# Upward MLP: 112 DMA issues move from SyncE's queue to ScalarE's

## The chip, the core and the metric

One Trainium2 chip, one of its cores. The metric is the device time of one launch in microseconds (us). Every execution is timed; one more is recorded by the hardware profiler, and its trace is what is read here. Engines: PE (TensorE), ACT (ScalarE), DVE (VectorE), POOL (GpSimd) and SP (SyncE, which here only issues DMAs).

## What is computed

A block of two layers on 1024 tokens of width 1024, in float32. Each layer has a mixer (layer 0: gated delta rule beside an RWKV-7 recurrence; layer 1: retention) and an MLP. The change is in the MLP:

```python
D_MODEL, SEQ, DEPTH = 1024, 1024, 2
D_FF = 4 * D_MODEL
...
for layer in range(DEPTH):
    u = rmsnorm(h, norm_mix_pre[layer])
    ...
    h = h + rmsnorm(mix, norm_mix_post[layer])
    u = rmsnorm(h, norm_mlp_pre[layer])
    f = jnp.square(jax.nn.relu(u @ mlp_w_up[layer])) @ mlp_w_down[layer]
    h = h + rmsnorm(f, norm_mlp_post[layer])
```

## The kernel before

Each matrix product of the MLP is made from seven products of half-size blocks instead of eight (a Strassen-Winograd scheme), and each fp32 operand is split in two parts for PE: the high one by a cast on ACT (L1183), the low one by a subtraction on DVE (L1184); three matmuls (L1315 to L1317, or L1467 to L1469) then make one product.

**Up part.** The 4096 columns of the hidden layer are worked in 16 steps p. For the first eight, `begin(p)` runs early, while the mixer before is still ending (this is called the front below): two products on PE, a copy of the first on ACT (L1335, tile x1, stored to `xds[p]`), and Relu and Square of the second on ACT (L1322, L1323), stored by `store(1, p, r)`. Then a loop runs over p in the order 0, 8, 1, 9, ... 7, 15. Each pass loads 1 MB of weights (L1307), makes sums on POOL, five or seven products on PE and sums on DVE (L1382, L1386, L1390, L1397, L1402), and again Relu and Square on ACT. Its results are the left operands of the down part's seven products: number 1, 2 and 4 come straight from ACT's Square; 3, 5, 6 and 7 are sums that POOL makes of them (L1405 to L1411). `store(n, p, r)` writes each to DRAM, 128 x 512 fp32, 256 KB: to `hds[n][p // 2]`, or, for n = 4 in layer 1, to `hq`.

**Down part.** For each product number and h from 0 to 7 it loads a pair of those results (`hds[n][h]`, L1535) and a block of `mlp_w_down` (L1437), splits both, and multiplies on PE. The sum on POOL in `right` (L1431) and the copies and sums in `flush` finish the scheme. The place where the last p of the up part and the first h of the down part overlap is called the seam below. There are two, one per layer: at about 1440 and 2930 us.

**What sets the order.** A scheduler orders the instructions of each engine beforehand; on the chip every engine runs its own stream in order. A DMA is an instruction in the stream of the engine that issues it. It signals one of eight completion semaphores, DMAHW0 to DMAHW7, given out in rotation over all DMAs of the program; a DMA whose semaphore is still in use by the one eight places before waits, on the engine that issues it, until that one has landed. In the kernel before, all stores and loads of the MLP stand in SP's stream.

Of the kernel before, what the change touches and what calls it, by code (L numbers as in the profile page):

```python
# [20 lines left out]
P = 128  # L21
# [88 lines left out]
def hybrid_block_kernel(  # L110
# [20 lines left out]
    PE, ACT, DVE, POOL, SP = nc.tensor, nc.scalar, nc.vector, nc.gpsimd, nc.sync  # L131
# [3 lines left out]
    def mk(pool, shape, tag, dt=F32, **kw):  # L135
        if isinstance(pool, Area):
            return pool.take(shape, tag, dt, **kw)
        uid[0] += 1
        return pool.tile(shape, dt, tag=tag, name=f"{tag}_{uid[0]}", **kw)
# [24 lines left out]
    hds = {n: [mk(dram, [P, 2, HT], f"hd{n}{i}") for i in range(8)] for n in range(1, 8)}  # L164
    hq = mk(dram, [P, 4, 16, P], "hq")
    xds = [mk(dram, [P, HT], f"xd{p}") for p in range(NB)]
# [1030 lines left out]
    def mlp(layer, res, mid, dst, late=()):  # L1197
# [7 lines left out]
        if True:  # L1205
# [92 lines left out]
            def tile_of(p, area):  # L1298

                raw = mk(area, [P, KT, P], "w0")  # L1300
                SP.dma_start(raw, mlp_w_up[layer][:, 2 * P * p : 2 * P * p + P].rearrange("(k p) c -> p k c", p=P))
                return raw[:, 0:4], raw[:, 4:8]

            def quads(p):

                raw = mk(raws, [P, KT, 2 * P], "raw")
                SP.dma_start(raw, mlp_w_up[layer][:, 2 * P * p : 2 * P * (p + 1)].rearrange("(k p) c -> p k c", p=P))  # L1307
                return {f"a{f + 1}{k + 1}": raw[:, 4 * k : 4 * k + 4, P * f : P * f + P] for f in range(2) for k in range(2)}
# [15 lines left out]

            def store(n, p, r):

                if n == 4 and layer:
                    SP.dma_start(hq[:, :, p, :], r.rearrange("p (t c) -> p t c", c=P))
                else:
                    SP.dma_start(hds[n][p // 2][:, p % 2, :], r)  # L1330

            def first_product(w, x, area=None):
                ps = mk(psu, [P, HT], "pu")
                product(ps, operand(w, area), b11, True, False)
                ACT.copy(x, ps)  # L1335
                return ps

            def first_output(p, ps, w, r, area=None):
                product(ps, operand(w, area), b21, False, True)
                squared(r, ps)  # L1340
                store(1, p, r)

            def begin(p, area, ops_area=None):

                wa, wb = tile_of(p, area)
                x = mk(keep, [P, HT], "x1")
                ps = first_product(wa, x, ops_area)
                SP.dma_start(xds[p], x)
                first_output(p, ps, wb, mk(keep, [P, HT], "r"), ops_area)

            firsts = region((88, 104)).area(4)
            for p in range(NB // 2):
                begin(p, firsts, early_ops)
            firsts = region((0, 16)).area(4)
            later = iter(range(NB // 2, NB))
            for t, n in ((4, 2), (5, 1), (6, 1), (7, 0)):
                next(run[t], None)
                for p in range(n):
                    begin(next(later), firsts)
# [5 lines left out]
            for p in ORDER:  # L1365
                q = quads(p)
# [23 lines left out]
                DVE.tensor_tensor(out=r22, in0=u3, in1=b5, op=ALU.add)  # L1390
                squared(r22, r22)
                store(4, p, r22)
                if p >= NB:
                    first_output(p, b1, q["a12"], r11)
                product(b7, operand(q["a22"]), ops["t4"], False, True)
                r12 = mk(res_, [P, HT], "r")
                DVE.tensor_tensor(out=r12, in0=u2, in1=b7, op=ALU.add)  # L1397
                squared(r12, r12)
                store(2, p, r12)
                product(b5, operand(S[:, 3]), ops["b22"], False, True)  # L1400
                r21 = mk(res_, [P, HT], "r")
# [486 lines left out]
```

## Time and profile before

| what | us |
|---|---|
| median of 3 runs | 3277.05 |
| their range | 3265.05 to 3279.01 |
| the profiled execution | 3272.72 |
| its span on the core | 3271.0 |
| PE busy | 3100.0 (95%) |
| DVE busy | 1996.6 (61%) |
| ACT busy | 1307.8 (40%) |
| POOL busy | 1243.3 (38%) |

DMA-issuing instructions are not counted as busy time. A busy PE is one with a matmul in flight; the granted clock says at what speed. An idle time of an engine costs nothing as long as another engine sets the pace, so the stretches are read one by one. The mean rate of all DMA over the span is 126 GB/s; the 40 us rows show how unevenly that is spread.

### The profile page before, as it was taken

How to read it: one execution, taken by the hardware profiler on the slowest of the kernel's cores; microseconds unless marked ns; L12 is line 12 of the kernel's file. 1: busy time of each engine (PE TensorE's matmuls, PEld its weight loads, DVE VectorE, ACT ScalarE, POOL GpSimd, SP SyncE). 2: the span in 40 equal slices, each digit the busy share in tenths (PEclk: the TensorE clock that was granted, in tenths of full speed). 3: DMA queues.
4: the chain of work that ended last, by engine and by line, in shares of the span. 5: the costliest groups of instructions: out<-in, count | busy, mean ns of one | idle time of the engine just before them, and what ended most of it. 6: DMA issues, size and time to landing. Idle time of an engine off the chain costs nothing. (4 is left out here: it accounts for less than half of the span.)

```text
span 3271.0 us, 44331 instructions
## 1 busy us (share of the span) xinstructions
PE 3100.0 (95%) x16424; PEld 2648.7 (81%) x16424; DVE 1996.6 (61%) x3427; ACT 1307.8 (40%) x2336; POOL 1243.3 (38%) x1549
## 2 busy tenths in 40 slices
PE   8889899899999889999999999999999989999998
PEld 6678787788788668878888899998999878877886
DVE  6445446555534865557578665667655675558585
ACT  5332333332323655544345333234432355553343
POOL 1664354454350067756150111112011057657060
PEclk9898879998979889999999999999999999999999
DMA  5221222221323545585354322344222456566354
GB/s 171 68 58 47 56 72 60 61 63 41 78 77 121 193 138 184 188 293 189 111 173 162 103 78 84 91 136 135 78 84 84 125 172 208 178 244 219 99 165 142
DMA packets 395609, 411.13 MB, mean 126 GB/s; under 512 B 69120, under 2 KB 303488, under 8 KB 394880
## 3 DMA queue, kind: packets, MB, share of 16 engines
q1 hardware_dynamic: 395392, 408.29, 39.7%
q8 instruction: 129, 2.11, 0.3%
q14 instruction: 88, 0.72, 0.1%
HBM read 312.28 MB, written 95.94 MB: 125 GB/s over the span
## 5 line engine op out<-in xcount | busy, mean ns | idle before, releaser
L185 PE MATMUL bank<-piece,piece 128*128 128x512 f32 (+7 forms) x10032 | 1740.7, 335 | 66.1 <-ACT piece L312 14.1
L185 PEld LDWEIGHTS bank<-piece,piece 128*128 128x128 f32 (+1 forms) x10032 | 1501.9, 199 | 273.2 <-issue 34.6
L1184 DVE TENSOR_TENSOR piece<-piece,piece 128x512 fp32r<-128x512 f32 (+2 forms) x436 | 596.4, 1394 | 191.7 <-ACT piece L1183 188.4
L1183 ACT CAST piece<-piece 128x512 fp32r<-128x512 f32 (+2 forms) x436 | 353.7, 838 | 548.0 <-PE bank L1468 207.0
L1315 PE MATMUL bank<-piece,piece 128*128 128x512 f32 x896 | 352.2, 394 | 20.4 <-ACT piece L1183 7.7
L1468 PE MATMUL bank<-piece,piece 128*128 128x512 f32 x896 | 352.0, 394 | 13.0 <-DVE piece L1184 13.0
L1316 PE MATMUL bank<-piece,piece 128*128 128x512 f32 x896 | 351.7, 393 | 1.9 <-DVE piece L1246 1.2
L1469 PE MATMUL bank<-piece,piece 128*128 128x512 f32 x896 | 351.0, 393 | 0.2 <-DVE piece L1184 0.2
L1317 PE MATMUL bank<-piece,piece 128*128 128x512 f32 x896 | 347.8, 392 | 0.9 <-DVE piece L1184 0.9
L205 DVE TENSOR_TENSOR piece<-piece,piece 128x1024 fp32r<-128x1024 f32 x202 | 258.4, 1280 | 130.4 <-ACT piece L204 129.1
L204 ACT CAST piece<-piece 128x1024 fp32r<-128x1024 f32 x204 | 213.5, 1047 | 284.6 <-PE bank L185 263.1
L1467 PE MATMUL bank<-piece 128*128 128x512 f32 x832 | 323.4, 392 | 2.5 <-ACT piece L1183 1.9
L1431 POOL TENSOR_TENSOR piece<-piece,piece 128x1024 f32<-128x1024 f32 (+1 forms) x72 | 215.0, 3005 | 263.4 <-DMA piece<-in_mlp_w_down_dram 207.5
L1596 POOL TENSOR_TENSOR piece<-piece,piece 128x512 f32<-128x512 f32 x32 | 64.6, 2018 | 605.9 <-DVE piece L1595 439.0
L621 POOL TENSOR_TENSOR piece<-piece 128x120 f32<-128x120 f32 (+22 forms) x496 | 186.6, 376 | 233.4 <-DMA piece<-dm 178.7
L1315 PEld LDWEIGHTS bank<-piece,piece 128*128 128x128 f32 x896 | 169.8, 190 | 58.6 <-ACT piece L1183 8.3
L1468 PEld LDWEIGHTS bank<-piece,piece 128*128 128x128 f32 x896 | 169.9, 190 | 50.8 <-DVE piece L1184 15.3
L625 POOL TENSOR_TENSOR piece<-piece,piece 128x120 f32<-128x120 f32 (+22 forms) x496 | 188.4, 380 | 37.4
L1316 PEld LDWEIGHTS bank<-piece,piece 128*128 128x128 f32 x896 | 170.0, 190 | 38.4 <-DVE piece L313 1.6
L1317 PEld LDWEIGHTS bank<-piece,piece 128*128 128x128 f32 x896 | 169.9, 190 | 36.7 <-DVE piece L1184 1.6
L1469 PEld LDWEIGHTS bank<-piece,piece 128*128 128x128 f32 x896 | 170.4, 190 | 36.0 <-DVE piece L1184 0.6
L1467 PEld LDWEIGHTS bank<-piece 128*128 128x128 f32 x832 | 157.2, 189 | 36.0 <-ACT piece L1183 2.3
(243 smaller groups left out, 3045.8 us busy)
## 6 DMA issues: line engine op xcount, KB each, us to landing
hd<-piece SPq DMA_DIRECT2D x208, 256.0 KB
piece<-hd SPq DMA_DIRECT2D x104, 512.0 KB
piece<-in_ret_w_in_dram SPq DMA_DIRECT2D x96, 512.0 KB
piece<-in_mlp_w_down_dram SPq DMA_DIRECT2D x80, 512.0 KB
piece<-in_mlp_w_up_dram SPq DMA_DIRECT2D x32, 1024.0 KB
piece<-in_ab_w_in_dram SPq DMA_DIRECT2D x60, 512.0 KB
piece<-in_ret_w_out_dram SPq DMA_DIRECT2D x32, 512.0 KB
h<-piece SPq DMA_DIRECT2D x24, 512.0 KB
```

The lines of the kernel that those rows point to most:

```text
L185: PE.matmul(ps, lhsT, rhs, start=start, stop=stop)
L204: ACT.copy(hi, raw)
L205: eng.tensor_tensor(out=lo, in0=raw, in1=hi, op=ALU.subtract)
L1183: ACT.copy(hi, src)
L1184: eng.tensor_tensor(out=lo, in0=src, in1=hi, op=ALU.subtract)
L1315: PE.matmul(ps, w[0][:, k, :], u[0][:, k, :], start=start and k == 0, stop=False, skip_group_check=True)
L1316: PE.matmul(ps, w[0][:, k, :], u[1][:, k, :], start=False, stop=False, skip_group_check=True)
L1317: PE.matmul(ps, w[1][:, k, :], u[0][:, k, :], start=False, stop=stop and k == 3, skip_group_check=True)
L1431: eng.tensor_tensor(out=out, in0=a, in1=b, op=op)
L1467: PE.matmul(ps, a[0], b[0], start=first, stop=False)
L1468: PE.matmul(ps, a[1], b[0], start=False, stop=False)
L1469: PE.matmul(ps, a[0], b[1], start=False, stop=last)
```

## The change

`store` picks ACT's queue for the results 1, 2 and 4, which ACT makes, and keeps SP's for 3, 5, 6 and 7, which POOL makes. `begin` stores x1, a copy made by ACT, from ACT's queue. Sizes, addresses and the number of DMAs stay. A line is added, so lines behind L1327 are one higher in the changed kernel.

```diff
             def store(n, p, r):
 
+                q = ACT if n in (1, 2, 4) else SP
                 if n == 4 and layer:
-                    SP.dma_start(hq[:, :, p, :], r.rearrange("p (t c) -> p t c", c=P))
+                    q.dma_start(hq[:, :, p, :], r.rearrange("p (t c) -> p t c", c=P))
                 else:
-                    SP.dma_start(hds[n][p // 2][:, p % 2, :], r)
+                    q.dma_start(hds[n][p // 2][:, p % 2, :], r)
...
                 x = mk(keep, [P, HT], "x1")
                 ps = first_product(wa, x, ops_area)
-                SP.dma_start(xds[p], x)
+                ACT.dma_start(xds[p], x)
                 first_output(p, ps, wb, mk(keep, [P, HT], "r"), ops_area)
```

ACT's stream grows from 2075 to 2187 rows, SP's shrinks from 1108 to 996. Apart from the 112 DMAs, the streams keep their order except for a few places, most of them in the fronts.

First the seam of layer 0 (p = 15), ACT's stream before. `piece_75` is the tile of a result, `piece_80` a block of the down weights, `piece_95` and `piece_96` high parts of it; `bank` is a product in PSUM.

```order
L1322 ACTIVATE piece_75_8484<-piece_75_8484 128x512 [waits DVE_49]
L1323 ACTIVATE piece_75_8484<-piece_75_8484 128x512 [waits Activation_49]
L1183 CAST piece_97_10314<-piece_81_10297 128x1024 [waits DMAHW2_49]
L1322 ACTIVATE piece_75_8484<-bank_7_75 128x512 [waits DMAHW4_49,PE_49,Pool_49]
L1183 CAST piece_95_10312<-piece_80_10296 128x1024 [waits DMAHW3_49]
L1323 ACTIVATE piece_75_8484<-piece_75_8484 128x512 [waits Activation_49]
L1183 CAST piece_96_10313<-piece_80_10296 128x1024 [waits DMAHW5_49]
L1322 ACTIVATE piece_75_8484<-piece_75_8484 128x512 [waits DVE_49]
L1323 ACTIVATE piece_75_8484<-piece_75_8484 128x512 [waits Activation_49]
```

The same place in the changed kernel; `hd_90`, `hd_66` and `hd_74` are the pairs `hds[4][7]`, `hds[1][7]` and `hds[2][7]`.

```order
L1322 ACTIVATE piece_75_8484<-piece_75_8484 128x512 [waits DVE_49]
L1323 ACTIVATE piece_75_8484<-piece_75_8484 128x512 [waits Activation_49]
L1183 CAST piece_97_10314<-piece_81_10297 128x1024 [waits DMAHW2_49]
L1331 DMA hd_90_158<-piece_75_8484 128x512 [waits DMAHW1_49,Activation_49]
L1322 ACTIVATE piece_75_8484<-bank_7_75 128x512 [waits DMAHW4_49,PE_49,Pool_49]
L1183 CAST piece_95_10312<-piece_80_10296 128x1024 [waits DMAHW3_49]
L1323 ACTIVATE piece_75_8484<-piece_75_8484 128x512 [waits Activation_49]
L1331 DMA hd_66_134<-piece_75_8484 128x512 [waits DMAHW6_49,Activation_49]
L1183 CAST piece_96_10313<-piece_80_10296 128x1024 [waits DMAHW5_49]
L1322 ACTIVATE piece_75_8484<-piece_75_8484 128x512 [waits DVE_49]
L1323 ACTIVATE piece_75_8484<-piece_75_8484 128x512 [waits Activation_49]
L1331 DMA hd_74_142<-piece_75_8484 128x512 [waits DMAHW7_49,Activation_49]
```

Three DMAs have come in between; each carries a wait for a DMAHW semaphore, and what follows it in ACT's stream starts after it. Which DMAs used these semaphores before shows in SP's stream of the kernel before, at the same place (`piece_94` is a load of the pair `hds[1][5]`, the other loads are blocks of the down weights):

```order
L1535 DMA piece_94_10310<-hd_64_132 128x1024 [waits DMAHW1_49]
L1330 DMA hd_102_170<-piece_74_8483 128x512 [waits DMAHW2_49,Pool_49]
L1330 DMA hd_78_146<-piece_75_8484 128x512 [waits DMAHW3_49,Pool_49]
L1437 DMA piece_83_10299<-in_mlp_w_down_dram 128x2x512 [waits DMAHW4_49,PE_49]
L1437 DMA piece_82_10298<-in_mlp_w_down_dram 128x2x512 [waits DMAHW5_49,PE_49]
L1437 DMA piece_82_10298<-in_mlp_w_down_dram 128x2x512 [waits DMAHW6_49]
L1437 DMA piece_83_10299<-in_mlp_w_down_dram 128x2x512 [waits DMAHW7_49]
L1437 DMA piece_103_10566<-in_mlp_w_down_dram 128x2x512 [waits DMAHW0_49,DVE_49]
L1330 DMA hd_90_158<-piece_75_8484 128x512 [waits DMAHW1_49,Activation_49]
```

In the changed kernel the last of these rows is gone from SP's stream and stands in ACT's; those above it stay on SP. The store of `hd_66` likewise follows eight places behind the second load of `piece_82`, on DMAHW6.

Last the seam of layer 1, ACT's stream in the changed kernel, with the hq store of p = 15 and the same pair `hd_66`:

```order
L1329 DMA hq_183<-piece_176_20159 512x1x128 [waits DMAHW4_49,Activation_49]
L1322 ACTIVATE piece_176_20159<-bank_7_75 128x512 [waits DMAHW1_49,PE_49,Pool_49]
L1323 ACTIVATE piece_176_20159<-piece_176_20159 128x512 [waits Activation_49]
L1183 CAST piece_195_21986<-piece_181_21971 128x1024 [waits DMAHW7_49]
L1331 DMA hd_66_134<-piece_176_20159 128x512 [waits DMAHW0_49,Activation_49]
L1183 CAST piece_196_21987<-piece_181_21971 128x1024 [waits DMAHW1_49]
```

Without the two DMA rows this is the order before; now the first cast is behind one DMA and the second behind two.

## Rows read from the trace of the kernel before

**Rows 1.** The page: the span.
```profile
span 3271.0 us, 44331 instructions
```

**Rows 2.** Busy time by stretch: us, busy time (instructions) of PE, PEld, DVE, ACT, POOL; granted clock, DMA share, GB/s.
```profile
1180.00:1220.00 40.00, 35.11 (x144) 28.69 (x145) 31.33 (x30) 19.50 (x34) 33.12 (x23) 0.88 0.42 133
1380.00:1420.00 40.00, 40.00 (x178) 33.11 (x177) 22.73 (x28) 20.98 (x34) 25.77 (x19) 1.00 0.54 184
1420.00:1460.00 40.00, 37.58 (x158) 30.34 (x157) 20.99 (x19) 16.92 (x24) 18.75 (x12) 0.96 0.93 343
2640.00:2680.00 40.00, 30.70 (x125) 23.14 (x124) 31.26 (x33) 21.53 (x40) 30.12 (x20) 0.93 0.52 174
2880.00:2920.00 40.00, 40.00 (x179) 33.10 (x178) 19.07 (x26) 20.65 (x34) 22.32 (x16) 1.00 0.55 184
2920.00:2960.00 40.00, 36.87 (x155) 29.82 (x154) 24.57 (x18) 17.86 (x23) 21.05 (x12) 0.96 1.02 382
```

**Rows 3.** The same for PE alone, 5 us in each seam.
```profile
1450.00:1455.00 5.00, 3.17 (x8) 0.78 1.05 394
2940.00:2945.00 5.00, 4.24 (x12) 0.66 1.05 384
```

**Rows 4.** Issues by source line: duration in ns, min/median/max; first and last start.
```profile
L1330 SPq DMA_DIRECT2D hd<-piece x208: 319/320/1289, 1133.8 to 2959.9; - x104
L1328 SPq DMA_DIRECT2D hq<-piece x16: 518/518/672, 2690.4 to 2938.1; - x16
```

**Rows 5.** Waits of SP, 1220 to 1420 us: us in total, times, longest.
```profile
SPq L1330 <- ACT piece L1323: 40.7, 23, 3.5
```

**Rows 6.** Timeline of SP's issues at seam 0: start us, us, engine, line.
```profile
1444.41 4.96 SPq L1437 DMA_DIRECT2D piece<-in_mlp_w_down_dram  x5
1450.85 0.34 SPq L1330 DMA_DIRECT2D hd<-piece  x1
1451.53 3.61 SPq L1437 DMA_DIRECT2D piece<-in_mlp_w_down_dram  x4
1456.17 1.69 SPq L1330 DMA_DIRECT2D hd<-piece  x2
```

**Rows 7.** Timeline of ACT at seam 0.
```profile
1443.62 0.59 ACT L1322 ACTIVATE piece<-bank 128x512 f32<-128x512 f32 x1
1444.11 1.04 ACT L1183 CAST piece<-piece 128x1024 fp32r<-128x1024 f32 x1
1445.05 0.63 ACT L1323 ACTIVATE piece<-piece 128x512 f32<-128x512 f32 x1
1445.71 1.05 ACT L1183 CAST piece<-piece 128x1024 fp32r<-128x1024 f32 x1
```

**Rows 8.** Timeline of DVE at seam 0; in brackets idle time before, and its releaser.
```profile
1446.79 1.23 DVE L1184 TENSOR_TENSOR piece<-piece,piece 128x1024 fp32r<-128x1024 f32 x1
1448.54 4.20 DVE L1184 TENSOR_TENSOR piece<-piece,piece 128x1024 fp32r<-128x1024 f32 x2 [0.52 <-PE bank L1316]
```

**Rows 9.** Timeline of PE at seam 0.
```profile
1451.65 0.96 PE L1468 MATMUL bank<-piece,piece 128*128 128x512 f32 x3 [2.25 <-DVE piece L1184]
```

**Rows 10.** Timeline of SP's issues at seam 1.
```profile
2938.08 0.52 SPq L1328 DMA_DIRECT2D hq<-piece  x1
...
2942.36 0.47 SPq L1330 DMA_DIRECT2D hd<-piece  x1
```

**Rows 11.** Timeline of ACT at seam 1.
```profile
2929.78 0.63 ACT L1323 ACTIVATE piece<-piece 128x512 f32<-128x512 f32 x1
...
2934.82 1.05 ACT L1183 CAST piece<-piece 128x1024 fp32r<-128x1024 f32 x1 [0.93 <-DMA piece<-in_mlp_w_down_dram]
```

**Rows 12.** Timeline of DVE at seam 1.
```profile
2935.91 1.23 DVE L1184 TENSOR_TENSOR piece<-piece,piece 128x1024 fp32r<-128x1024 f32 x1 [1.45 <-ACT piece L1183]
```

**Rows 13.** Timeline of PE at seam 1.
```profile
2940.76 1.92 PE L1468 MATMUL bank<-piece,piece 128*128 128x512 f32 x4 [2.48 <-DVE piece L1184]
```

**Rows 14.** Waits of PE in layer 1's front, 2640 to 2680 us: us in total, times, longest.
```profile
PE bank L1315 <- ACT piece L1245: 3.6, 2, 3.1
...
PE bank L1315 <- ACT piece L1335: 1.7, 1, 1.7
```

## The prediction

> **What bounds the kernel now.** I read the page first: a span of 3271.0 us on one core [rows 1]. Then the table of busy time by stretch, 40 us a line [rows 2]. In the middle of both up parts TensorE (PE) is busy 40.00 of 40 us at a granted clock of 1.00, while ScalarE (ACT) works some 21 of 40: there PE is the limit, and ACT may lose time without anyone noticing. At the two seams, where the up part ends and the down part begins, the row differs: PE is busy 37.58 and 36.87 of 40, and the DMA engines are full, at a share of 0.93 and 1.02. The 5 us rows inside the seams show 1.05 with 394 and 384 GB/s [rows 3]. So a DMA lands late exactly there, and whatever waits for a landing waits long. The moved stores are therefore followed in three places: steady stretch, seams, and the fronts of the up parts (1180 to 1220 and 2640 to 2680 us), where PE also has holes.
>
> **What moves.** 112 DMAs leave SP's queue for ACT's: 16 of xds and 96 stores of n = 1, 2, 4 (80 go to hds, 16 to hq). The order of instructions shows them on ACT, each right behind its Square or copy or one or two instructions later, with the semaphore waits they had on SP. One issue costs SP 319 ns, 518 ns for hq [rows 4]. ACT's own price for issuing is not in this trace; I take SP's, with 0 and twice that as bounds. That is 96 x 0.32 + 16 x 0.52 = 39 us on ACT.
>
> **Steady stretch: nothing.** SP's waits between 1220 and 1420 say that these stores wait for Square itself, 23 times, 3.5 us at most [rows 5]: the DMA eight places back has landed by then, so ACT will not wait either. What is left is the issue, 48 per up part of some 270 us, so seven or 2.3 us in 40, against 19 us of free ACT time [rows 2]. Cover: ACT's idle time and PE being full. Were that cover gone, the bound would be the whole 39 us; as ACT's load only goes from 52% to some 58%, I count 0. What SP saves, it has no use for while PE is full: 0 as well.
>
> **Seam 0: +10.3.** A DMA may start only when the one eight places earlier, on the same completion semaphore, has landed. SP shows the price: it is through with its five loads at 1449.37, yet issues the next store at 1450.85; it is through with four more at 1455.14, and the store of n = 1 leaves at 1456.17 [rows 6], although its Square ended at 1445.68 [rows 7]. On SP that delayed only SP. Now the same two waits stand in ACT's stream, ahead of casts. Forward: the n = 4 store waits until 1450.8 and takes 0.34, so 1451.2; Relu 0.6, the first cast 1.04 and Square 0.63 [rows 7] bring 1453.4; the n = 1 store waits for the second load of piece_82, which by SP's own wait lands at about 1456.1, and is issued by 1456.5; the cast behind it (1.05) ends at 1457.6. Before, it ended at 1446.76 [rows 7]. VectorE (DVE) takes this cast's result in its next instruction but one: its subtraction started at 1446.79, 0.03 after the cast [rows 8]; there is no slack. It takes 1.23, to 1458.9. The next subtraction, first of a pair of 4.20, feeds PE: from 1448.54 it ran until PE began at 1451.65 [rows 8, 9], so 3.1, and PE begins at 1462.0. Shift: 1462.0 - 1451.65 = 10.3. If that subtraction runs at the 1.23 of the other, because nothing else works then, it is 8.5. Lower end 6 (the loads land 4 us sooner, since SP is no longer held up among them), upper end 12 (a second full wait of the n = 2 store, partly over by then).
>
> **Seam 1: +7.9.** Here hq's Square ends at 2930.41 [rows 11], but hq leaves only at 2938.08 and the n = 1 store at 2942.36 [rows 10]. On ACT: 2938.6 after hq's issue, then Relu, Square and a cast, 2.3, to 2940.9; the n = 1 store waits to 2942.3 and takes 0.47; the cast behind it ends at 2943.8 instead of 2935.87 [rows 11]. DVE starts 0.04 after that cast [rows 12], again with no slack, and PE's next group waits for DVE [rows 13]: +7.9. Lower end 4, upper end 9, by the same two doubts.
>
> Neither is made up later: PE is what the rest of the layer waits for.
>
> **Clock: +1.** After its 2.25 us hole at 1451.65 PE's granted clock is 0.78 in the mean of 5 us [rows 3, 9], and 0.66 after the one at 2940.76: part of the stretch runs at 1.2 GHz instead of 2.4. That price is paid already; a longer hole may lengthen it. By the rows, 5 us at 0.78 and 0.66 lose 1.1 and 1.7 us: ends 0 and +2.8, taken +1.
>
> **Fronts: +1.** Eight begin() per layer put 16 issues of 0.32 on ACT, 5.1 us per layer, 10.2 in all if each is on the path. ACT is busy 19.5 and 21.5 of 40 there [rows 2], so I take a tenth. On the other side PE loses 3.6 us in layer 1's front to ACT's L1245 copy [rows 14]; stores that leave earlier on a queue of their own could return that at most. Ends -3.6 and +10.2.
>
> Sum: 10.3 + 7.9 + 1 + 1 + 0 = 20.2. The profiled execution took 3272.72 us, 4.3 below the median of the runs and inside their 3265.05 to 3279.01. 3272.7 + 20.2 = **3293 us**.
>
> What speaks for another reading is the full DMA queue. The rows show that both seams run at 384 to 394 GB/s [rows 3], so where a store is issued adds no bandwidth. The Trainium skill, page "DMA: Bandwidth & Descriptors", section "Issuing engines are not separate DMA queues", says that DMAs started from different engines run on the same 16 DMA engines, interleaved, and that issuing from several saves only the sequencer's time to start them, usually small. By that rule alone the change comes out at no difference, 3273 instead of 3293. The seam rows agree with its first half (shared engines), but show beside it where a wait stands.
>
> **Rivals.**
> *Nothing changes, 3273 (chance 0.24), not slower.* Mechanism: SP, freed of 112 issues and their waits, sends the down part's loads some us earlier, so that the DMA eight places back has landed when ACT reaches its store. Place: the n = 1 store at each seam. It decides if the landing comes before 1445.7 and 2932.4, 10 us earlier than SP's rows show. For it: SP's own waits at the seam delay the loads behind them [rows 6]. Against it: DMA is full there already [rows 3], and earlier issues then land no sooner. Then only the +1 of the fronts remains, 3272.7 + 0 to 1. The page's rule above ends here too; it has no chance beyond this one.
> *Relief at the fronts, faster, 3268 (0.06).* If the seam waits vanish as above and the stores of begin() leave without standing behind 1 MB loads in SP's queue, PE gets back the 3.6 us of L1245 and 1.7 of L1335 [rows 14]: 3272.7 - 5.3 = 3267.4. All of PE's idle time in that front is 40 - 30.7 = 9.3 [rows 2]. Against: both conditions must hold.
> *Issue on ACT is on the path at the fronts too, 3302 (0.10).* Seams as forecast, but ACT's chain of copy, cast and Square is what PE waits for in both fronts: +10.2 instead of +1. For it: the releasers of rows 14 are ACT's. Against: ACT is only half busy.
> That the change would not do what it says is ruled out by the order: the 112 rows did change engine.
>
> **How the numbers follow.** Forecast (both seam stalls): 0.60. Its own range is 6 + 4 + 0 - 3.6 = +6 to 12 + 9 + 2.8 + 2 = +26, most of it between +13 and +23. A measurement of this kernel can tell about 0.5%, 16.4 us, from no change; the forecast lies only 3.8 above that line (3273 + 16.4 = 3289.1), so I give it 0.7 of its chance as slower and 0.3 as no difference. Slower: 0.60 x 0.7 + 0.10 = 0.52. Same: 0.60 x 0.3 + 0.24 + 0.03 = 0.45. Faster by over 16.4 us none of the cases reaches; 0.03 of the relief's chance goes there for what I priced too low. The range runs from 3272, so that the no-change case is held, to 3305 above the last rival; the relief and the ends of the bounds stay out.
>
> **What would show it.** Right: in the rows by stretch PE's busy time at 1420 to 1460 falls from 37.58 to about 28, and at the second seam from 36.87 to about 29; ACT shows a DMA issue whose wait ends at about 1456 and DVE's L1184 starts some 10 us later; the steady rows keep 40.00. Wrong: PE's seam rows unchanged with ACT's stores issued at once behind Square (first rival), PE's front rows up (second) or down by several us (third), or any steady row of PE under 39.5, which would mean that an issue on ACT costs far more than on SP.

## The result, and the profile after

| | us |
|---|---|
| before, median of 7 runs | 3277.05 (3265.05 to 3292.82) |
| changed, median of 7 runs | 3301.89 (3298.33 to 3311.27) |
| ratio | 1.0075, 95% interval 1.0056 to 1.0093 |
| span of the profiled execution, before and changed | 3271.0 and 3300.1 |

The changed kernel is slower by 0.75%, some 25 us. Busy time by stretch of the changed kernel; columns as in [rows 2]:

```profile
1380.00:1420.00 40.00, 40.00 (x178) 33.14 (x177) 25.63 (x28) 19.06 (x32) 29.48 (x22) 1.00 0.54 169
1420.00:1460.00 40.00, 39.25 (x174) 32.16 (x172) 16.08 (x20) 17.98 (x27) 14.43 (x11) 1.00 0.81 297
1460.00:1500.00 40.00, 28.56 (x109) 22.41 (x110) 21.57 (x13) 13.54 (x16) 21.70 (x10) 0.79 0.92 332
...
2920.00:2960.00 40.00, 40.00 (x178) 33.10 (x178) 16.68 (x23) 18.05 (x29) 17.07 (x13) 1.00 0.74 263
2960.00:3000.00 40.00, 28.44 (x103) 21.19 (x101) 22.09 (x13) 15.29 (x18) 24.98 (x10) 0.80 0.92 345
```

The steady row is what it was: PE 40.00 of 40. The rows that differ are those of the two seams, which in this profile fall 10.5 and 24 us later than in [rows 2]; PE is idle there for 11 us and more, at a granted clock of 0.79 and 0.80.

**What ACT's issues cost, and which of them wait.** The lines of the changed kernel's stores, by source line, as in [rows 4]:

```profile
L1331 ACTq DMA_DIRECT2D hd<-piece x80: 321/326/623, 1143.0 to 2973.9; - x80
L1329 ACTq DMA_DIRECT2D hq<-piece x16: 527/527/584, 2714.5 to 2962.1; - x16
```

ACT pays what SP paid: 326 ns against 320, 527 against 518. Of the 112 moved stores 107 are issued within 0.2 us of the end of the ACT instruction that made their data, nearly all after 0.03 us. Five wait: n = 4 and n = 1 at the first seam (8.4 and 3.4 us), and n = 4, 1 and 2 at the second (7.6, 2.0 and 4.5). Each of the five starts within 0.1 us of the landing of the DMA eight places before it. All five belong to p = 15.

Timeline of ACT at the first seam, changed kernel; `ACTq` is a DMA issue:

```profile
1453.21 1.03 ACT L1183 CAST piece<-piece 128x1024 fp32r<-128x1024 f32 x1
1461.67 0.33 ACTq L1331 DMA_DIRECT2D hd<-piece  x1
1462.12 0.60 ACT L1322 ACTIVATE piece<-bank 128x512 f32<-128x512 f32 x1 [7.88 <-DMA piece<-in_mlp_w_down_dram]
1462.61 1.04 ACT L1183 CAST piece<-piece 128x1024 fp32r<-128x1024 f32 x1
1463.55 0.63 ACT L1323 ACTIVATE piece<-piece 128x512 f32<-128x512 f32 x1
1467.57 0.33 ACTq L1331 DMA_DIRECT2D hd<-piece  x1
1467.94 1.04 ACT L1183 CAST piece<-piece 128x1024 fp32r<-128x1024 f32 x1 [3.76 <-DMA piece<-in_mlp_w_down_dram]
```

In [rows 7] Relu, cast, Square and cast run back to back within 3.2 us; here two DMA issues stand among them, each behind a wait whose releaser is a DMA of the down part. DVE and PE at the same place:

```profile
1469.02 5.66 DVE L1184 TENSOR_TENSOR piece<-piece,piece 128x1024 fp32r<-128x1024 f32 x3 [11.76 <-ACT piece L1183]
```

```profile
1463.70 1.65 PE L1468 MATMUL bank<-piece 128*128 128x512 f32 x3 [4.45 <-ACT piece L1183]
1471.43 1.65 PE L1469 MATMUL bank<-piece,piece 128*128 128x512 f32 x3 [6.08 <-DVE piece L1184]
1474.73 0.80 PE L1470 MATMUL bank<-piece,piece 128*128 128x512 f32 x1 [1.66 <-DVE piece L1184]
```

DVE sits idle for 11.76 us until the cast is there, PE for 4.45, 6.08 and 1.66 where it lost 2.25 [rows 9] and 0.17 before. And the DMA engines are full through all of it, at a share of 1.04 to 1.06, as before [rows 3]; PE by 5 us:

```profile
1455.00:1460.00 5.00, 4.25 (x19) 1.00 1.04 399
1460.00:1465.00 5.00, 1.30 (x3) 0.69 1.04 394
1465.00:1470.00 5.00, 0.35 (x1) 0.50 1.05 396
1470.00:1475.00 5.00, 1.92 (x4) 0.50 1.06 401
```

**Where the two profiles drift apart.** I set the start of DVE's k-th instruction in one profile against that in the first profile of the kernel before, and read the lag at points of time of that first profile. The table holds the experiments too, which are told below:

| profile | lag at 1130 us | seam 0: lag at 1435, 1510 | gained there | seam 1: lag at 2925, 3010 | gained there | both seams |
|---|---|---|---|---|---|---|
| changed | 9.8 | 10.5, 22.3 | +11.8 | 24.1, 30.0 | +5.9 | 17.7 |
| seam's stores back on SP | 4.0 | 6.4, 6.3 | -0.1 | 7.3, 6.9 | -0.4 | -0.5 |
| only the seam's stores on ACT | 6.2 | 7.7, 19.2 | +11.5 | 16.8, 23.2 | +6.4 | 17.9 |
| all on ACT, seam's behind the casts | 10.9 | 13.1, 13.0 | -0.1 | 14.1, 17.2 | +3.1 | 3.0 |
| n = 1 of the seam on SP | 6.8 | 9.3, 16.5 | +7.2 | 16.9, 23.4 | +6.5 | 13.7 |
| fronts only | 17.1 | 18.1, 16.6 | -1.5 | 18.0, 17.5 | -0.5 | -2.0 |
| kernel before again | 17.5 | 17.3, 16.9 | -0.4 | 19.3, 19.4 | +0.1 | -0.3 |

Of the 29.1 us between the two spans 9.8 are there at 1130 us, where the first moved DMA is about to be issued. That part needed a test of its own (below: the kernel before again).

### The profile page after: what moved, and what is told of

Read it like the earlier page. It is cut to its first block, busy times and chain, and to the rows that moved or that the text cites. A ratio compares the mean times of both kernels' runs of the same rounds, so it can differ in the third digit from the quotient of the medians.

```text
span 3300.1 us, 44304 instructions
## 1 busy us (share of the span) xinstructions
PE 3113.8 (94%) x16424; PEld 2656.3 (80%) x16424; DVE 1990.0 (60%) x3427; ACT 1308.8 (40%) x2336; POOL 1238.7 (38%) x1549
## 3 DMA queue, kind: packets, MB, share of 16 engines
q8 instruction: 129, 2.11, 0.3%
## 5 line engine op out<-in xcount | busy, mean ns | idle before, releaser
L1469 PE MATMUL bank<-piece,piece 128*128 128x512 f32 x896 | 352.3, 394 | 13.8 <-DVE piece L1184 13.8
L1468 PE MATMUL bank<-piece 128*128 128x512 f32 x832 | 325.8, 395 | 13.4 <-ACT piece L1183 10.7
L1469 PEld LDWEIGHTS bank<-piece,piece 128*128 128x128 f32 x896 | 170.2, 190 | 52.7 <-DVE piece L1184 17.7
L1468 PEld LDWEIGHTS bank<-piece 128*128 128x128 f32 x832 | 158.1, 190 | 48.2 <-ACT piece L1183 12.0
```

Of the source, the lines that this page charges most:

```text
L1468: PE.matmul(ps, a[0], b[0], start=first, stop=False)
L1469: PE.matmul(ps, a[1], b[0], start=False, stop=False)
```

## The experiments

Theory W: the loss is the wait of the last p's stores, put in ACT's stream ahead of casts that DVE and PE need at once. Rivals: issuing on ACT costs wherever it happens (I); two queues make the loads late (Q); the slower clock ahead of the change belongs to it (C).

**1. The seam's stores back on SP** (6 of 112 DMAs).

```diff
-                q = ACT if n in (1, 2, 4) else SP
+                q = ACT if n in (1, 2, 4) and p < 2 * NB - 1 else SP
```

> As the changed kernel, but the three stores of the last step (p = 15; n = 1, 2, 4) go back to SP's queue, in both layers: 6 of 112 DMAs. Theory W (the wait at the seam): the loss sits in the waits of these six on ACT, so it goes: 3277 us within 5, ratio to before 0.998 to 1.003; TensorE's holes at the seams shrink to those of the kernel before (2.3 and 2.5 us before L1469). Rival I (issue on ACT costs everywhere): 106 of 112 issues stay, so 3300 within 3. Rival Q (stores on a second queue push the loads back): the loads of the seam are late still, 3295 to 3300. Rival C (the slower clock between 1040 and 1080 us in the profile of the changed kernel belongs to the change): about 3287, and the profile shows it again.

Measured: 3281.14 us (12 runs) beside 3279.15 for the kernel before (29 runs, which serve experiments 1 to 4); ratio 1.0007, interval 0.9985 to 1.0030; both as expected. With 106 of 112 issues still on ACT the loss is gone. PE at the two seams, timeline:

```profile
1457.89 0.96 PE L1469 MATMUL bank<-piece,piece 128*128 128x512 f32 x3 [2.10 <-DVE piece L1184]
...
2948.06 2.08 PE L1469 MATMUL bank<-piece,piece 128*128 128x512 f32 x4 [2.48 <-DVE piece L1184]
```

These are the holes of the kernel before, 2.25 and 2.48 [rows 9, 13]. Rival I falls: the interval allows the 106 issues 9.8 us at most, and the profile shows none of it at the seams.

**2. The reverse: only the seam's stores on ACT.**

```diff
-                q = ACT if n in (1, 2, 4) else SP
+                q = ACT if n in (1, 2, 4) and p == 2 * NB - 1 else SP
...
-                ACT.dma_start(xds[p], x)
+                SP.dma_start(xds[p], x)
```

> The reverse: only the three stores of the last step (p = 15) go by ACT's queue, in both layers; the other 106 DMAs stay on SP. Theory W: nearly the whole loss, 3277 + 11.8 + 7.8 = 3297 within 5, ratio 1.004 to 1.008; the profile shows ACT waiting 7 to 9 us ahead of the store of n = 4 at both seams. Rival I: 6 of 112 issues, 3278. Rival Q: 3278 to 3285, since six stores move. Rival C: nothing of a clock loss ahead of 1100 us can come from it, as the program is that of before up to 1400 us.

Measured: 3303.64 us (9 runs), 1.6 above the range expected; ratio 1.0070, as expected, interval 1.0047 to 1.0094. Six DMAs make the whole loss. PE's timeline at the first seam repeats that of the changed kernel hole by hole, and the lag gained at both seams is 17.9 against 17.7:

```profile
1460.79 1.65 PE L1468 MATMUL bank<-piece 128*128 128x512 f32 x3 [4.41 <-ACT piece L1183]
1468.49 1.65 PE L1469 MATMUL bank<-piece,piece 128*128 128x512 f32 x3 [6.06 <-DVE piece L1184]
1471.80 0.80 PE L1470 MATMUL bank<-piece,piece 128*128 128x512 f32 x1 [1.66 <-DVE piece L1184]
```

**3. All on ACT, but the seam's stores behind the casts.** This parts the queue from the place in the stream. The stores of p = 15 are collected and emitted in the down part, with an edge of order behind the casts of its second and third step (`cast` lists the casts so far, `held` the stores put off):

```diff
+                if q is ACT and p == 2 * NB - 1 and held is not None:
+                    held.append((n, p, r))
+                    return
...
                     a, b = split_in(ring, sh, raw, "op"), split_in(ring, sh, right(n, h), "op")
+                    if n == 1 and h == 2:
+                        todo, held = held, None
+                        with tc.issue_after(cast[-1]), tc.issue_after(cast[-3]):
+                            for x in todo:
+                                store(*x)
```

> All 112 DMAs on ACT's queue as in the changed kernel, but the three stores of the last step are put behind the casts of the down part's first three steps in ACT's stream (an edge of order, no wait added); what they wait for and the queue they use stay. Theory W: the place in the stream is what costs, so the loss goes: 3278 within 5, ratio 0.998 to 1.004; ACT still waits some us ahead of these stores, but TensorE's holes at the seams are those of the kernel before. Rivals I and Q: nothing is taken back, 3297 to 3302.

Measured: 3287.96 us (12 runs), 5 above the range expected; ratio 1.0021, inside 0.998 to 1.004, interval 1.0005 to 1.0037: most of the loss is gone, not all. ACT and PE at the first seam (lines are shifted: the cast is L1185, the store L1339, Relu L1325, PE's group L1477):

```profile
1458.65 1.03 ACT L1185 CAST piece<-piece 128x1024 fp32r<-128x1024 f32 x1
1468.16 1.74 ACTq L1339 DMA_DIRECT2D hd<-piece  x2
1469.94 0.63 ACT L1325 ACTIVATE piece<-piece 128x512 f32<-128x512 f32 x1 [10.26 <-DMA piece<-in_mlp_w_down_dram]
```

```profile
1464.58 0.97 PE L1477 MATMUL bank<-piece,piece 128*128 128x512 f32 x3 [2.11 <-DVE piece L1187]
```

ACT sits idle for 10.26 us here, longer than at any one place in the changed kernel's seams, on the same queue for the same kind of landing: the first store is issued 8.5 us after the cast, where the changed kernel's n = 4 store waits 8.4. (The kernel before has an idle time of ACT here too, 5.31 us for DVE, one Relu and Square later; a part of this wait takes its place.) And PE loses 2.11 as in the kernel before. So it is not the wait as such, nor the queue (rival Q falls), but what stands behind the wait. At the second seam 3.1 us stay, by the table; there PE's later hole is 4.8 us long instead of 3.6. PE, DVE and POOL at that hole (L1187 is the subtraction, L1440 POOL's sum in `right`):

```profile
2987.42 0.79 PE L1477 MATMUL bank<-piece,piece 128*128 128x512 f32 x1 [4.79 <-DVE piece L1187]
2974.75 13.76 DVE L1187 TENSOR_TENSOR piece<-piece,piece 128x1024 fp32r<-128x1024 f32 x5 [1.90 <-ACT piece L1185]
2973.97 12.32 POOL L1440 TENSOR_TENSOR piece<-piece,piece 128x1024 f32<-128x1024 f32 x4
```

DVE's subtractions take 13.76 us for five while POOL's sums run beside them; in the same trace those with nothing on POOL beside them take 1.21 to 1.23 each. Which instruction behind the three stores brings the two together there was not tried; the 0.21% is somewhat more than the 3.0 us that the table shows.

**4. Only the store of n = 1 back on SP at the seam.**

```diff
-                q = ACT if n in (1, 2, 4) else SP
+                q = ACT if n in (1, 2, 4) and (n, p) != (1, 2 * NB - 1) else SP
```

> As the changed kernel, but only the store of n = 1 of the last step goes back to SP (2 of 112). Theory W: the wait of the n = 4 store stays, that of the n = 1 store (3.4 and 2.0 us) and its issue go from ACT: at the first seam the second cast of the pair starts 3.8 us sooner, at the second 1.5, so the seams cost 8.0 + 6.3 = 14.3 instead of 19.6 and the time falls by about 5, to 3293 to 3297. Rivals I and Q: 3300.

Measured: 3296.43 us (7 runs), as expected; ratio 1.0056, interval 1.0035 to 1.0077. The seams gain 7.2 + 6.5 = 13.7 where 8.0 + 6.3 = 14.3 was expected. At the first one PE's 6.08 us hole shrinks while the other two stay:

```profile
1462.32 1.65 PE L1468 MATMUL bank<-piece 128*128 128x512 f32 x3 [4.27 <-ACT piece L1183]
1466.18 1.65 PE L1469 MATMUL bank<-piece,piece 128*128 128x512 f32 x3 [2.21 <-DVE piece L1184]
```

So at the first seam the two waits add up singly: the n = 4 store makes the hole before L1468, the n = 1 store that before L1469. The second seam does not show it in the sum: 6.5 are gained here, 5.9 in the changed kernel. PE there, changed kernel and this one:

```profile
2964.95 1.65 PE L1468 MATMUL bank<-piece 128*128 128x512 f32 x3 [4.39 <-ACT piece L1183]
2969.32 0.79 PE L1468 MATMUL bank<-piece 128*128 128x512 f32 x1 [2.72 <-DVE piece L1403]
```

```profile
2959.26 1.65 PE L1468 MATMUL bank<-piece 128*128 128x512 f32 x3 [5.94 <-ACT piece L1183]
2962.06 0.79 PE L1468 MATMUL bank<-piece 128*128 128x512 f32 x1 [1.15 <-DVE piece L1403]
```

The second hole shrinks by 1.6 us without the n = 1 store, but the n = 4 store waits 9.1 us instead of 7.6 and the first hole grows by as much; why its landing came later is open. The runs alone would not part this kernel from the changed one (the intervals overlap); the profile does, at the first seam.

**5. The kernel before once more**, for the 9.8 us that stand ahead of the change.

> The kernel before itself, profiled once more, to see what one profile differs from the next without any change. In the profiles of the changed kernel and of the first four experiments TensorE's clock is 0.50 to 0.58 between 1040 and 1080 us, where the first profile of the kernel before has 0.88, and they run 11 to 13 us behind it by 1230 us, ahead of any seam. If that belongs to the single profile (chance), this one shows a clock of about 0.5 to 0.6 there and a span some 5 to 10 us over 3271. If it belongs to the change, it shows 0.88 again and a span near 3271.

Measured: 3294.17 us (1 run), span 3292.5; the kernel before had a median of 3289.49 (13 runs) in the same series. Experiments 5 and 6 ran on another chip than 1 to 4, and lay 10 us higher altogether. Busy time of all engines at 1040 to 1080 us, first profile of the kernel before, the changed kernel, and the kernel before again:

```profile
1040.00:1080.00 40.00, 28.47 (x207) 25.46 (x206) 22.74 (x81) 14.25 (x63) 0.00 (x0) 0.88 0.30 106
```

```profile
1040.00:1080.00 40.00, 39.96 (x182) 35.87 (x180) 11.96 (x34) 7.82 (x45) 0.00 (x0) 0.57 0.11 34
```

```profile
1040.00:1080.00 40.00, 40.00 (x205) 35.78 (x203) 10.76 (x29) 6.01 (x32) 0.00 (x0) 0.70 0.04 13
```

The same program that had a clock of 0.88 has 0.70 there, and lags 17.5 us at 1130. That is neither the 0.5 to 0.6 and the 5 to 10 us that were expected of chance nor the 0.88 and 3271 of the other case. But rival C falls: between the DVE instructions that stand at 1040 and 1080 us in the first profile all seven later profiles lose 12.2 to 12.9 us, this one 12.3 and that of experiment 2 12.3 as well, whose engines run the same instructions as the kernel before up to the first seam. So this is not the change; the first profile was a quick one. At its seams, the second profile gains -0.4 and +0.1, so the table's gains elsewhere are good to about half a us; the fronts-only kernel, with -1.5, says one and a half.

**6. The fronts only** (the x1 copies and n = 1 for p below 8 on ACT, all else on SP).

```diff
-                q = ACT if n in (1, 2, 4) else SP
+                q = ACT if n == 1 and p < NB else SP
```

> Only the 32 DMAs of begin() (the x1 copies and the stores of n = 1 for p below 8) go by ACT's queue; all others stay on SP. Theory W: no wait there is long, so nothing: 3278 within 5, ratio 0.997 to 1.003. Rival I (issue on ACT is on the path at the fronts): +10, 3288. Relief at the fronts: -5, 3273.

Measured: 3282.77 us (10 runs) beside 3289.49; ratio 0.9988, interval 0.9968 to 1.0008, as expected. No difference that can be told. The interval, -10.5 to +2.6 us, excludes the 10 us of rival I; it leaves room for the 5 us of the relief, and does not show them.

## Why the prediction came out as it did

3293 us were forecast, slower, with 0.52 for over 0.5%; 3301.89 were measured, inside 3272 to 3305. The mechanism was the one forecast, and the two seams carry it: 17.7 us in the profile, where the forecast's seam and clock terms were 19.2. In the rows that hold the seams PE is busy 28.56 and 28.44 of 40 us, where about 28 and 29 were named as the sign. That the sum came so near is in part luck: the second seam's term was too large (7.9, where PE's holes grew by 3.5), and the clock's too small (1, where about 4.4 are left for it).

*Steady stretch: 0.* Right. PE is at 40.00 there, and all 74 loop stores ahead of p = 15 that go from ACT leave within 0.2 us. ACT's price for an issue, which I had to take from SP, is SP's.

*Seam 0: +10.3.* Right in the chain, with two errors of opposite sign. The cast behind the n = 1 store ended at 1468.98; before, moved by the lag of 10.5, it would have been 1457.26: 11.7 later, not 10.8, as the landing came 0.9 us later than SP's rows let expect. DVE's second subtraction took less than the 3.1 I carried over: from DVE's start at 1469.02 to PE's at 1471.43 it is 2.4 for both, where I had 1.23 + 3.1. That is the lower bound I had named. PE's group began 1471.43 - 1451.65 - 10.5 = 9.3 us late, and the seam came to 11.8.

*Clock: +1 for both seams.* Too small. The other 2.5 us of the first seam arise after that group's start. 1.5 of them are PE's third hole, 1.66 where the kernel before has 0.17: it waits for DVE's third subtraction, which took 3.4 us beside a sum on POOL. The rest is slower matmuls: the clock is at 0.50 (the 1.2 GHz level) from 1465 to 1475 and at 0.60 in the five us after, with three holes of 4.45, 6.08 and 1.66 around them, where one hole of 2.25 went with 0.78 [rows 3]. Over each whole seam PE's holes grow from 2.4 to 12.2 us and from 8.6 to 12.0, that is by 9.8 of the 11.8 gained and by 3.5 of the 5.9. What is left, 2.0 and 2.4, is the price of the lower clock, an estimate by difference and no better than the table it is made from: 4.4 us in all, beyond the upper end of 2.8. I had priced one longer hole, and overlooked the one that the n = 4 store opens before L1468: the first cast of the pair is late as well, not only the second.

*Seam 1: +7.9, "neither is made up later".* The first half is right, the second is what failed. The chain: ACT's issues and PE's next groups at this seam, changed kernel:

```profile
2962.05 0.53 ACTq L1329 DMA_DIRECT2D hq<-piece  x1
...
2966.00 0.32 ACTq L1331 DMA_DIRECT2D hd<-piece  x1
```

```profile
2972.29 2.07 PE L1469 MATMUL bank<-piece,piece 128*128 128x512 f32 x4 [2.18 <-DVE piece L1184]
2997.68 1.92 PE L1468 MATMUL bank<-piece 128*128 128x512 f32 x4 [1.86 <-ACT piece L1183]
3000.48 0.79 PE L1469 MATMUL bank<-piece,piece 128*128 128x512 f32 x1 [0.89 <-DVE piece L1184]
```

PE's group starts 2972.29 - 2940.76 - 24.1 = 7.4 us late. But 25 us on, the kernel before has a hole that is shorter now; its timeline:

```profile
2965.35 1.19 PE L1467 MATMUL bank<-piece 128*128 128x512 f32 x4 [1.86 <-ACT piece L1183]
2970.14 0.79 PE L1468 MATMUL bank<-piece,piece 128*128 128x512 f32 x1 [3.60 <-DVE piece L1184]
```

3.60 became 0.89, and of 7.4 only 5.9 were left at 3010 us, the lower clock's price included. I had put this hole on PE's own chain, so that it would shift along unchanged; part of it hangs on something that did not shift. The traces show what changed beside it. DVE's three subtractions ahead of this hole and POOL's two sums, kernel before:

```profile
2964.38 6.84 DVE L1184 TENSOR_TENSOR piece<-piece,piece 128x1024 fp32r<-128x1024 f32 x3 [0.87 <-ACT piece L1183]
2962.64 6.37 POOL L1431 TENSOR_TENSOR piece<-piece,piece 128x1024 f32<-128x1024 f32 x2 [0.20 <-issue]
```

The same in the changed kernel:

```profile
2996.71 4.85 DVE L1184 TENSOR_TENSOR piece<-piece,piece 128x1024 fp32r<-128x1024 f32 x3 [3.07 <-ACT piece L1183]
2992.58 5.63 POOL L1432 TENSOR_TENSOR piece<-piece,piece 128x1024 f32<-128x1024 f32 x2 [1.89 <-DVE piece L1184]
```

Before, POOL works until 2969.01, beside the first two subtractions, and the three take 6.84 us. In the changed kernel POOL is through at 2998.21, only the first has POOL beside it, and the three take 4.85: 2.0 of the 2.7 us by which the hole shrank. That POOL's work is what slows DVE is read from these rows and was not tried.

*Fronts: +1.* (The sum of the range's upper end took +2 for this term, where its own line names +10.2; only the third rival held that case.) Nothing, as near as can be seen: between 2600 and 2740 us the changed kernel loses 1.3 us of its lag, and the kernel with unchanged fronts (experiment 2) loses 1.7. Experiment 6 agrees. The third rival's 10 us are excluded, the relief's 5 are not by the runs alone.

*The first rival* (SP, freed, sends the loads earlier, so that the landing is there in time) fails as its own counter-argument said. SP's row at the first seam of the changed kernel:

```profile
1454.89 11.04 SPq L1438 DMA_DIRECT2D piece<-in_mlp_w_down_dram  x9
```

Nine loads go out without a store between them, yet they are spread over 11 us, because each waits for a landing (7.7 us of waits in all), and the DMA engines are at 1.04 to 1.06 throughout. Another issuing engine adds no bandwidth there, but that does not make it no difference: the wait moves with the DMA, and here that is all that counts. The page "DMA: Bandwidth & Descriptors" of the Trainium skill (section "Issuing engines are not separate DMA queues") says that DMAs started from any of these engines run on the same 16 DMA engines. The trace agrees: the share at the seam was 1.05 with all issues on SP and 1.04 to 1.06 with some on ACT.

*The distance that is left.* 3301.9 - 3293 = 8.9 us. 4.3 of them are the start: the sum was made against the profiled execution, and that lay below the median, as all later profiles show for the stretch at 1050 us. The rest is not settled. The 17.7 us of the profile lie just below the interval of the runs (0.56 to 0.93% of 3277 are 18.4 to 30.5), and experiments 1 to 4, which share one set of runs of the kernel before, all measure by their ratios 3 to 5 us more than their seams show.

## What to carry to other kernels

A DMA that waits for an earlier landing holds everything behind it on the engine that issues it. Moving an issue from a queue engine, which has nothing else to do, to a compute engine is free where the landing is long there (107 of 112 stores here), and costs up to the whole wait where the DMA engines are full and the next instruction feeds the critical engine (8.4 + 3.4 us of waits and 11.8 us lost at the first seam, 7.6 + 2.0 and 5.9 at the second). So look for the few places with full DMA, and there keep the issue where it waits alone, or put it behind the work that others need.

## What the runs showed of the hardware

A store that waited 8.5 us on ACT cost nothing (experiment 3, first seam), and one that waited 3.4 us on the same engine cost about 4 us of PE's time (experiment 4): the length of a wait says little without its place.

DVE's subtraction of 128 x 1024 took 1.21 to 1.23 us wherever POOL had nothing to do beside it (113 times in the changed kernel's profile), and 1.21 to 3.43 us, with a median of 2.9, where POOL worked all the while (38 times). That it is POOL's work that slows it was not tried.

And one and the same program ran a stretch of 40 us at a granted clock of 0.88 in one execution and of 0.70 in another (0.50 to 0.58 with the changed kernel and experiments 1 to 4), and fell 12.3 us behind in it; a difference of two single profiles is to be read stretch by stretch before it is put down to a change.
